# Row sums on one core: contiguous 8 MB loads, and early sums stored in 64-byte runs behind the last loads

## Chip, cores, metric

One core of one Trainium2 chip; the other cores are idle. The metric is the device time of one execution in microseconds (us).

## The reference

```python
batch, seq, dim = 32, 512, 1024
x = np.random.randn(batch, seq, dim).astype(np.float32)     # 67.1 MB
return np.sum(x, axis=-1)                                   # 16,384 sums, 64 KB
```

## The kernel before

Partition p takes 112 successive rows in a first block, then 16 in a last one, always 16 rows (64 KB a partition, 8 MB in all) a load. So in the first seven groups the reads of two neighbouring partitions lie 448 KB apart (below: the pitch); in the last group they lie 64 KB apart, and that group is contiguous.

```python
BLOCKS = (112, 16)
G = 16
...
xpool = ctx.enter_context(tc.tile_pool(name="x", bufs=3))
...
for b, n in enumerate(BLOCKS):
    # x_b: x_flat[r0 : r0 + P*n] as "(p c) d -> p (c d)"; out_b alike
    x_b, out_b, res = block(done * P, n)
    ...
        parts = (0, 1, m) if done + c == 0 else (0, m)       # group 1: one row first, then 15
        for i, k in zip(parts, parts[1:]):
            nc.sync.dma_start(out=xt[:, i * D : k * D], in_=x_b[:, (c + i) * D : (c + k) * D])
        ...                                                  # sums: VectorE; 7 of group 7's rows ScalarE
    if not final:
        for i, k in ((0, 104), (104, P)):                    # 448-byte runs, ScalarE's queue
            nc.scalar.dma_start(out=out_b[i:k], in_=res[i:k])
...
# last group: loads of 9, 4, 2 rows, then 544 and 480 columns of the last row (SyncE's queue)
# sums on both engines, then
nc.sync.dma_start(out=out_b, in_=res)                        # 64-byte runs
```

The first two loads are moved ahead of the start barrier.

Of the kernel before, what the change touches and what calls it, by code (L numbers as in the profile page):

```python
# [1 line left out]

# [4 lines left out]

F32 = mybir.dt.float32
ADD = mybir.AluOpType.add
COPY = mybir.ActivationFunctionType.Copy  # L10
X = mybir.AxisListType.X

BLOCKS = (112, 16)
G = 16
ACT_ROWS = 7
CUT = 544
EARLY = 2


@with_exitstack  # L20
def row_sums(
    ctx: ExitStack,
    tc: tile.TileContext,
    x: bass.AP,
    out: bass.AP,
):
    nc = tc.nc
    P = nc.NUM_PARTITIONS

    x_flat = x.flatten_outer_dims()  # L30
    R, D = x_flat.shape
    C = R // P
    assert R % P == 0 and sum(BLOCKS) == C
    out_flat = out.rearrange("a (b c) -> (a b c)", c=1)

    xpool = ctx.enter_context(tc.tile_pool(name="x", bufs=3))
    rpool = ctx.enter_context(tc.tile_pool(name="res", bufs=1))
    part = rpool.tile([P, 1], F32, name="part")
    seen = rpool.tile([P, 1], F32, name="seen")
    pairs = [rpool.tile([P, D // 2], F32, name=f"pairs{i}") for i in range(3)]  # L40

    def rows_dve(xt, res, j, n, c):
        nc.vector.tensor_reduce(  # L43
            out=res[:, c : c + n],
            in_=xt[:, j * D : (j + n) * D].rearrange("p (j d) -> p j d", d=D),
            axis=X,
            op=ADD,
        )

    def sum_act(v, acc):  # L50
        nc.scalar.activation(out=v, in_=v, func=COPY, accum_out=acc)  # L51

    def rows_act(xt, res, j, n, c):
        for i in range(n):
            sum_act(xt[:, (j + i) * D : (j + i + 1) * D], res[:, c + i : c + i + 1])

    def pairs_dve(xt, a, b, first, acc, pairs):
        h = (a + b) // 2
        nc.vector.tensor_tensor_reduce(  # L59
            out=pairs[:, 0 : h - a], in0=xt[:, a:h], in1=xt[:, h:b], scale=1.0, scalar=first,  # L60
            op0=ADD, op1=ADD, accum_out=acc,
        )

    def block(r0, n):
        x_b = x_flat[r0 : r0 + P * n].rearrange("(p c) d -> p (c d)", p=P)
        out_b = out_flat[r0 : r0 + P * n].rearrange("(p c) -> p c", p=P)
        return x_b, out_b, rpool.tile([P, n], F32, name=f"res{r0}")

    full = C - G
    done = 0  # L70
    for b, n in enumerate(BLOCKS):
        x_b, out_b, res = block(done * P, n)
        final = b == len(BLOCKS) - 1
        whole = n - G if final else n
        c = 0
        while c < whole:
            m = min(G, whole - c)
            xt = xpool.tile([P, G * D], F32, tag="xt", name="xt")
            parts = (0, 1, m) if done + c == 0 else (0, m)
            for i, k in zip(parts, parts[1:]):  # L80
                nc.sync.dma_start(
                    out=xt[:, i * D : k * D], in_=x_b[:, (c + i) * D : (c + k) * D]
                )
            a = ACT_ROWS if done + c + m == full else 0
            rows_dve(xt, res, 0, m - a, c)
            rows_act(xt, res, m - a, a, c + m - a)
            c += m
        if not final:

            for i, k in ((0, 104), (104, P)):  # L90
                nc.scalar.dma_start(out=out_b[i:k], in_=res[i:k])
        done += n

    xt = xpool.tile([P, G * D], F32, tag="xt", name="xt")
    cuts = [0, 9, 13, 15]
    for i, k in zip(cuts, cuts[1:]):
        nc.sync.dma_start(out=xt[:, i * D : k * D], in_=x_b[:, (c + i) * D : (c + k) * D])  # L97
    last = 15 * D
    for i, k in ((0, CUT), (CUT, D)):
        nc.sync.dma_start(  # L100
            out=xt[:, last + i : last + k],
            in_=x_b[:, c * D + last + i : c * D + last + k],
        )

    for i, k in zip(cuts[:2], cuts[1:3]):
        h = (k - i) // 2
        rows_dve(xt, res, i, h, c + i)
        rows_act(xt, res, i + h, k - i - h, c + i + h)
    pairs_dve(xt, 13 * D, 14 * D, 0.0, res[:, c + 13 : c + 14], pairs[2])
    rows_act(xt, res, 14, 1, c + 14)  # L110
    pairs_dve(xt, last, last + CUT, 0.0, part, pairs[0])


    nc.vector.tensor_copy(out=seen, in_=part)  # L114
    pairs_dve(xt, last + CUT, last + D, part, res[:, c + 15 : c + 16], pairs[1])
    nc.sync.dma_start(out=out_b, in_=res)


def kernel(tc: tile.TileContext, x: bass.AP, out: bass.AP):
    row_sums(tc, x, out)  # L120
    tc.close()
    tc.compile()  # L122



    sp = mybir.EngineType.SP
    fn = tc.nc.m.functions[0]
    entry, body = None, None
    for blk in fn.blocks:
        ops = [i for i in blk.instructions if i.engine == sp]  # L130
        if entry is None:
            entry = blk
        elif any(i.opcode == "DMACopy" for i in ops):
            body = blk
            break
    code = list(body.instructions)
    loads = [i for i in code if i.engine == sp][:EARLY]
    for load in loads:
        assert load.opcode == "DMACopy" and not load.sync_info.on_wait
        code.remove(load)  # L140
    body.instructions = code
    code = list(entry.instructions)
    at = next(k for k, i in enumerate(code) if i.engine == sp and i.opcode == "Drain")
    code[at:at] = loads
    entry.instructions = code

# [1 line left out]
_INS = ['x']  # L148
_OUTS = [((32, 512), 'float32')]


# [23 lines left out]
```

## Time and profile before

| | before |
|---|---|
| median of six runs | 162.13 us (162.03 to 162.42) |
| span in the profile | 160.6 us |
| DMA engines on loads | 97.2% of the span |
| VectorE busy | 76% |
| from one group's landing to the next | 19.37 us, 433 GB/s |
| group one landed | 21.98 us |

What bounds the kernel, with the lines of the page, is in the prediction. The trace also records each DMA packet (its queue, start, duration and bytes, but not which of the 16 engines ran it) and each of the 16 completions of a load. "Landed" below is the last of a load's completions, in us from the span's start.

### The profile page before, as it was taken

How to read it: one execution, taken by the hardware profiler on the slowest of the kernel's cores; microseconds unless marked ns; L12 is line 12 of the kernel's file. 1: busy time of each engine (PE TensorE's matmuls, PEld its weight loads, DVE VectorE, ACT ScalarE, POOL GpSimd, SP SyncE). 2: the span in 40 equal slices, each digit the busy share in tenths (PEclk: the TensorE clock that was granted, in tenths of full speed). 3: DMA queues.
4: the chain of work that ended last, by engine and by line, in shares of the span. 5: the costliest groups of instructions: out<-in, count | busy, mean ns of one | idle time of the engine just before them, and what ended most of it. 6: DMA issues, size and time to landing. Idle time of an engine off the chain costs nothing.

```text
span 160.6 us, 120 instructions
## 1 busy us (share of the span) xinstructions
DVE 121.4 (76%) x16; ACT 17.2 (11%) x31; POOL 0.2 (0%) x4
## 2 busy tenths in 40 slices
DVE  0000059997799958999499994999949999598884
ACT  0000000000000000000000000000000000596892
POOL 0000000000000000000000000000000000000000
DMA  9997996996996996996996979979969969998991
GB/s 375 490 398 337 490 522 294 490 522 261 522 506 278 522 506 278 522 506 278 522 506 278 522 326 457 522 310 473 522 294 490 522 261 522 432 432 369 410 402 62
DMA packets 2169, 67.18 MB, mean 418 GB/s; under 512 B 505, under 2 KB 633, under 8 KB 889
## 3 DMA queue, kind: packets, MB, share of 16 engines
q1 hardware_dynamic: 2016, 67.12, 97.2%
q10 hardware_dynamic: 153, 0.06, 0.1%
HBM read 67.11 MB, written 0.07 MB: 418 GB/s over the span
## 4 chain that ended last, share of the span: by engine, by line
DMA 75%; DVE 22%; SPq 0%; issue 0%; DVEq 0%
DMA xt<-in_x_dram 75%; DVE res L43 21%; DVE pairs L59 1%; SPq L97 0%; DVE seen L114 0%; DVE part L59 0%; DVEq L122 0%; DVE res L59 0%
## 5 line engine op out<-in xcount | busy, mean ns | idle before, releaser
L43 DVE TENSOR_REDUCE res<-xt 128x16 f32<-128x16384 f32 (+3 forms) x9 | 119.8, 13309 | 36.6 <-DMA xt<-in_x_dram 36.6
L51 ACT ACT_TABLE_LOAD x1 | 1.3, 1283 | 138.3 <-DMA xt<-in_x_dram 138.3
L51 ACT ACTIVATE xt<-xt 128x1024 f32<-128x1024 f32 x15 | 15.6, 1042 | 2.2 <-DMA xt<-in_x_dram 2.2
L51 ACT ACTIVATION_READ_ACCUMULATOR xt<-xt 128x1 f32 x15 | 2.8, 186 | 0.0
L59 DVE CUSTOM_DVE_ANT_0 pairs<-xt 128x512 f32<-128x512 f32 (+1 forms) x2 | 1.1, 566 | 0.3 <-DMA xt<-in_x_dram 0.3
L59 DVE CUSTOM_DVE_ANT_0 pairs<-xt,part 128x240 f32<-128x240 f32 x1 | 0.5, 467 | 0.0
L114 DVE COPY seen<-part 128x1 f32<-128x1 f32 x1 | 0.2, 153 | 0.0
L59 DVE DVE_READ_ACCUMULATOR2_ANT res<- 128x1 f32 x2 | 0.2, 81 | 0.0
L159 POOL MEMSET const-bfloat16-1.0<- 128x1 bf16 x1 | 0.1, 101 | 0.0
L159 POOL MEMSET const-uint8-127<- 128x1 uint8 x1 | 0.1, 101 | 0.0
L159 POOL MEMSET const-float32-0.0<- 128x1 f32 x1 | 0.1, 98 | 0.2 <-issue 0.2
L159 POOL MEMSET const-float32-1.0<- 128x1 f32 x1 | 0.1, 98 | 0.0
L59 DVE DVE_READ_ACCUMULATOR2_ANT part<- 128x1 f32 x1 | 0.1, 84 | 0.0
## 6 DMA issues: line engine op xcount, KB each, us to landing
xt<-in_x_dram SPq DMA_DIRECT2D x1, 7680.0 KB
xt<-in_x_dram SPq DMA_DIRECT2D x1, 4608.0 KB, 32.4
xt<-in_x_dram SPq DMA_DIRECT2D x1, 2048.0 KB, 36.9
xt<-in_x_dram SPq DMA_DIRECT2D x1, 1024.0 KB, 39.0
xt<-in_x_dram SPq DMA_DIRECT2D x1, 512.0 KB, 3.9
xt<-in_x_dram SPq DMA_DIRECT2D x1, 272.0 KB, 39.1
xt<-in_x_dram SPq DMA_DIRECT2D x1, 240.0 KB, 38.9
xt<-in_x_dram SPq DMA_DIRECT2D x6, 40.9
```

The lines of the kernel that those rows point to most:

```text
L43: nc.vector.tensor_reduce(out=res[:, c : c + n], in_=xt[:, j * D : (j + n) * D].rearrange("p (j d) -> p j d", d=D), axis=X, op=ADD,)
L51: nc.scalar.activation(out=v, in_=v, func=COPY, accum_out=acc)
L59: nc.vector.tensor_tensor_reduce(out=pairs[:, 0 : h - a], in0=xt[:, a:h], in1=xt[:, h:b], scale=1.0, scalar=first, op0=ADD, op1=ADD, accum ...
L114: nc.vector.tensor_copy(out=seen, in_=part)
L159: nc = _bacc.Bacc("TRN2", target_bir_lowering=False, num_devices=1)
```

## The change

Its intent: every load is one unbroken 8 MB of HBM, and the stores leave ScalarE and the middle of the load stream. The price is that group g's 16 sums of a partition are 64 bytes in the output, 8 KB from those of the next group.

```diff
-BLOCKS = (112, 16)
...
+    x_g = x_flat.rearrange("(b p c) d -> b p (c d)", p=P, c=G)
+    out_g = out_flat.rearrange("(b p c) -> p b c", p=P, c=G)
+    res = rpool.tile([P, C], F32, name="res")
...
+        for i, k in ((0, 1), (1, G)) if b == 0 else ((0, G),):
+            nc.sync.dma_start(out=xt[:, i * D : k * D], in_=x_g[b, :, i * D : k * D])
...
-            for i, k in ((0, 104), (104, P)):
-                nc.scalar.dma_start(out=out_b[i:k], in_=res[i:k])
...  (after the last group's loads)
+    for i, k in ((0, 4), (4, B - 1)):
+        nc.sync.dma_start(out=out_g[:, i:k], in_=res_g[:, i:k])
...
-    nc.sync.dma_start(out=out_b, in_=res)
+    nc.sync.dma_start(out=out_g[:, B - 1], in_=res[:, c:C])
```

More of the change, by code (lines that the diff above doesn't have):

```diff
@@ L32, in row_sums @@
     C = R // P
-    assert R % P == 0 and sum(BLOCKS) == C
+    assert R % P == 0 and C % G == 0
     out_flat = out.rearrange("a (b c) -> (a b c)", c=1)
@@ L62, in pairs_dve @@
         )
-    def block(r0, n):
-        x_b = x_flat[r0 : r0 + P * n].rearrange("(p c) d -> p (c d)", p=P)
-        out_b = out_flat[r0 : r0 + P * n].rearrange("(p c) -> p c", p=P)
-        return x_b, out_b, rpool.tile([P, n], F32, name=f"res{r0}")
-    full = C - G
-    done = 0
-    for b, n in enumerate(BLOCKS):
-        x_b, out_b, res = block(done * P, n)
-        final = b == len(BLOCKS) - 1
-        whole = n - G if final else n
-        c = 0
-        while c < whole:
-            m = min(G, whole - c)
-            xt = xpool.tile([P, G * D], F32, tag="xt", name="xt")
-            parts = (0, 1, m) if done + c == 0 else (0, m)
-            for i, k in zip(parts, parts[1:]):
-                nc.sync.dma_start(
-                    out=xt[:, i * D : k * D], in_=x_b[:, (c + i) * D : (c + k) * D]
-                )
-            a = ACT_ROWS if done + c + m == full else 0
-            rows_dve(xt, res, 0, m - a, c)
-            rows_act(xt, res, m - a, a, c + m - a)
-            c += m
-        if not final:
-            for i, k in ((0, 104), (104, P)):
-                nc.scalar.dma_start(out=out_b[i:k], in_=res[i:k])
-        done += n
+    x_g = x_flat.rearrange("(b p c) d -> b p (c d)", p=P, c=G)
+    out_g = out_flat.rearrange("(b p c) -> p b c", p=P, c=G)
+    B = C // G
+    res = rpool.tile([P, C], F32, name="res")
+    for b in range(B - 1):
+        xt = xpool.tile([P, G * D], F32, tag="xt", name="xt")
+        for i, k in ((0, 1), (1, G)) if b == 0 else ((0, G),):
+            nc.sync.dma_start(out=xt[:, i * D : k * D], in_=x_g[b, :, i * D : k * D])
+        a = ACT_ROWS if b == B - 2 else 0
+        rows_dve(xt, res, 0, G - a, b * G)
+        rows_act(xt, res, G - a, a, (b + 1) * G - a)
+    c = (B - 1) * G
+    x_b = x_g[B - 1]
     xt = xpool.tile([P, G * D], F32, tag="xt", name="xt")
@@ L96, in row_sums @@
     for i, k in zip(cuts, cuts[1:]):
-        nc.sync.dma_start(out=xt[:, i * D : k * D], in_=x_b[:, (c + i) * D : (c + k) * D])
+        nc.sync.dma_start(out=xt[:, i * D : k * D], in_=x_b[:, i * D : k * D])
     last = 15 * D
@@ L101, in row_sums @@
             out=xt[:, last + i : last + k],
-            in_=x_b[:, c * D + last + i : c * D + last + k],
+            in_=x_b[:, last + i : last + k],
         )
+    res_g = res.rearrange("p (b c) -> p b c", c=G)
+    for i, k in ((0, 4), (4, B - 1)):
+        nc.sync.dma_start(out=out_g[:, i:k], in_=res_g[:, i:k])
     for i, k in zip(cuts[:2], cuts[1:3]):
```

## The prediction

> **What bounds the kernel now.** I read the views in this order: the busy time by engine, the 40 slices, the stretches between two loads, the chain of waits and the timeline of the end, then the trace's record of each DMA packet.
>
> The page first. The columns of the last line are the rates of the 40 slices.
>
> ```profile
> DVE 121.4 (76%) x16; ACT 17.2 (11%) x31; POOL 0.2 (0%) x4
> ...
> DMA  9997996996996996996996979979969969998991
> GB/s 375 490 398 337 490 522 294 490 522 261 522 506 278 522 506 278 522 506 278 522 506 278 522 326 457 522 310 473 522 294 490 522 261 522 432 432 369 410 402 62
> ...
> q1 hardware_dynamic: 2016, 67.12, 97.2%
> q10 hardware_dynamic: 153, 0.06, 0.1%
> ```
>
> VectorE is busy for 76% and the 16 DMA engines for 97% of the span, nearly all of it on the loads (q1). The digits 6 and 7 and rates that swing between 261 and 522 look like gaps, but are an effect of the slices: a packet holds up to 64 KB, and its bytes are counted in the slice where it is recorded. Stretches from one load's landing to the next (bounds taken from the starts of VectorE's big sums) show it. Columns: stretch and length, busy time of the three engines, clock, DMA share, GB/s.
>
> ```profile
> 41.35:60.72 19.37, 17.22 (x2) 0.00 (x0) 0.00 (x0) 1.00 1.00 433
> 60.72:80.09 19.37, 17.22 (x1) 0.00 (x0) 0.00 (x0) 1.00 1.00 433
> ...
> 138.27:157.80 19.53, 17.60 (x8) 17.19 (x31) 0.00 (x0) 1.00 0.95 402
> ```
>
> A group of 16 rows a partition lands every 19.37 us, with the DMA engines busy all the time. VectorE needs 17.22 us for it and waits 2.15 us each time. The last stretch (402 GB/s) is not slower: 8.39 MB in 19.53 us are 430 GB/s; its first packets were recorded in the stretch ahead. The packets confirm this: a 65,536-byte packet takes 2.418 us (median of 768), and each engine carries eight a group, 8 x 2.418 = 19.34 us, so there is no gap between packets.
>
> The end of the chain of waits (start, length, what):
>
> ```profile
> 117.65 38.95 DMA xt<-in_x_dram
> 156.60 0.02 issue
> 156.62 0.69 DVE pairs L59
> 157.32 0.01 DVE res L59
> 157.32 0.36 DVE pairs L59
> 157.68 0.02 DVE part L59
> 157.70 0.02 issue
> 157.73 0.15 DVE seen L114
> 157.88 0.41 DVE pairs L59
> 158.29 0.01 DVEq L122
> ```
>
> And in the timeline of the end, the last store:
>
> ```profile
> 158.36 0.35 SPq L116 DMA_DIRECT2D out_dram<-res  x1
> ```
>
> The last load lands by the packet records at 157.81, VectorE sums its 240 pairs and the store of the last group's sums goes out at 158.36. Its first packet starts at 159.21, its last completion is recorded at 159.79, and the span ends at 160.6. So the time is: about 1.0 us to the first packet, some 157 us of loads at the engines' full rate, and a tail of 2.8 us. Only something that changes the packets' rate, the slowest engine's work, or this tail can change the end.
>
> **What the Trainium skill says.** All four places are on "DMA: Bandwidth & Descriptors".
> - "Where 436 GB/s comes from" (in "Bandwidth") gives 435.2 GB/s as the ceiling of 16 ports. The trace agrees: 433 GB/s in an undisturbed stretch. A better order of reads in HBM has half a per cent to win at most.
> - "Latency and other measured facts" lists that a pitch from partition to partition of 512 KiB and more, at powers of two, slows copies, and advises padding or tiles laid out contiguously. The first seven loads now have a pitch of 448 KB and get 64 KB. 64 KB is a power of two but below the listed sizes. The trace already has it: the last group of the kernel before is a contiguous 8 MB with 64 KB pitch. Its packets of 36,864 bytes took 1.364 us, 27.0 bytes a ns, against 27.1 for the 65,536-byte ones at 448 KB pitch. That small gap is a fixed cost of about 9 ns a packet, which the two sizes give together.
> - "Specifications" says that transfers under 512 B make the DMA engine read, modify and write. The last store has 64-byte runs already. Its 128 packets are recorded with 8 to 11 ns each, and successive ones on one engine start about 7 ns apart. So no such cost shows there, though that is only 8 packets an engine.
> - "Queues, rings and completion order" says that one engine consumes descriptors in ring order, and that the completion write lands only after every earlier write of that engine. So a slow early store can hold up a later one's completion. Nothing in this trace tests that.
>
> **The change, part by part.**
>
> 1. Loads of the first seven groups: same count, bytes and packets (64 KB a partition), other addresses. By the last group's evidence 0 us; I allow 0.2 us either way, mainly for the first 4 KB packets, which take up to 0.94 us while the transfers start.
>
> 2. The two stores from ScalarE's queue go. They were 128 packets of 448 bytes at 25 ns in the last group. Their 25 completion packets show that they ran on 13 and 12 engines, up to 10 packets an engine. From the landing of the group before to that of the last, the engine that lands first took 19.72 us, the one that lands last 19.55 us. So these stores delayed the engines that were ahead by about 0.17 us and apparently left the slowest alone. The 0.19 us by which the slowest exceeds 19.36 is the cutting of the last load in five: the packet times sum to 2.451 us instead of 2.418 us, eight times, so 0.26 us, about right. Removing the stores wins 0 to 0.05 us. The 0.98 us that ScalarE's queue spent issuing them lay in a wait for data (ACT idles 2.19 us until 149.20).
>
> 3. The new stores: 4 x 128 and 3 x 128 runs of 64 bytes, 896 packets on 16 engines, 56 an engine and two completions. Building the changed kernel shows their place: both on SyncE's queue after the last load, ahead of the last store. The first needs no fresh wait (the load ahead has already waited for its sums). The second waits for group seven's sums on both engines, about 147 us as now. Both are thus issued some 10 us before the loads end, and lie behind them in the same rings. They start on an engine when its last load packet ends, 157.39 on the slowest. At 7 to 14 ns (recorded spacing, and double it) 58 packets take 0.4 to 0.8 us, until 157.8 to 158.2. The last store cannot start before 159.21, because its sums aren't there. The hole between the loads and the last store is 159.21 - 157.39 = 1.82 us, and the new stores fit in it up to 1.82 / 58 = 31 ns a packet. So 0 us on the path; I allow 0.1 us for issue.
>
> 4. VectorE and ScalarE do the same instructions with the same shapes. Writing into one tile of sums brings no new wait: in the built kernel, the sums of the last group wait only for their loads, as before.
>
> Sum: 0 (loads) - 0.02 (old stores) + 0.05 (new stores) = +0.03 us. Predicted 162.1 us.
>
> **The rivals.**
>
> - Short writes to HBM are slow when there are many. Eight packets an engine may be absorbed by a buffer and 56 not. For it: only the last store shows such packets, and the skill warns of them. Against: 7 ns apart, and completion 0.37 us after the last packet. At 60 ns a packet the stores end at 157.39 + 58 x 0.06 = 160.9, the last store comes 1.7 us later, and the time is 163.8. To be slower by 2% (165.3 us), 3.2 us more are needed, so (1.82 + 3.2) / 58 = 87 ns a packet, eight to twelve times the recorded spacing.
> - The queue fills: the long row of descriptors behind the loads stops SyncE's issue, and the last store goes out late. Against: the loads drain from 149 on, and the last store is issued only at 158.36. If it had to wait for room it would cost some tenths, 162.5.
> - The 64 KB pitch makes the engines collide in HBM when seven groups run so. Against: the last group. Were 1% lost, it would be seven times 0.19, +1.4 us: 163.5.
> - Contiguous reads gain. The floor is 433 to 435 GB/s, 0.5% of 155 us, so -0.7 us at the very best: 161.4. The unbroken rows of packets speak against it.
>
> **Range and chances.** The runs of before lie within 0.11 us. Below, only the start and a hair of rate can win: 161.6. Above, the first three rivals in mild form add up to 0.9 us: 163.0. Faster by over 2% (under 158.9) is beyond the ceiling of the transfers: 0.01. Slower by over 2% needs the first rival in strong form, or two per cent of load rate: 0.04. The rest, 0.95, is within 2%.
>
> **What would show it right or wrong.** Right: stretches of 19.37 us at 433 GB/s; the old stores' queue gone and q1 with 896 64-byte packets and 32 completions more; these packets between about 157 and 158.3; the last store's instruction near 158.4 with 1.4 us to landing. Wrong: longer stretches or longer 65,536-byte packets (step 1, the pitch); small packets beyond 159.2 or the last store with more than 1.4 us to landing (step 3, short writes); SyncE's last issue well after VectorE's last sum (the queue); sums of the last group waiting for a store (step 4).

## More of the kernel before

All runs quoted here are at full clock. The experiments, e1 to e12, ran on four different chips, so each ratio compares only runs of the same rounds on one chip; the kernel before had medians of 162.04 to 162.23 us there.

## The result, and the profile after

| | before | after |
|---|---|---|
| median of six runs | 162.13 us | 162.77 us (162.55 to 163.01) |
| span in the profile | 160.6 us | 161.2 us |
| group one landed | 21.98 us | 22.41 us |
| last load landed | 157.80 us | 158.43 us |

The ratio is 1.0037 (95% interval 1.0024 to 1.0051): within 2%, but a real loss of 0.6 us. Ratios are the mean time of one kernel's fast runs over that of the other's of the same rounds, so not quite the ratio of the medians quoted. The profiled run of the changed kernel was its slowest of six (163.01); that of the kernel before, at 162.37 us, was also above its median.

From the page of the changed kernel, its slices and queues; q10, the queue of ScalarE's stores, is gone, and q1 has 928 packets more (896 of 64 bytes and 32 completions):

```profile
DMA  9979997997997997997998998998998999998992
...
q1 hardware_dynamic: 2944, 67.18, 97.5%
```

The stretches from one landing to the next, as read in the kernel before:

```profile
41.78:61.14 19.36, 17.22 (x2) 0.00 (x0) 0.00 (x0) 1.00 1.00 433
61.14:80.54 19.40, 17.22 (x1) 0.00 (x0) 0.00 (x0) 1.00 1.01 432
80.54:100.02 19.48, 17.22 (x2) 0.00 (x0) 0.00 (x0) 1.00 1.00 431
...
138.76:158.43 19.67, 17.74 (x8) 17.16 (x31) 0.00 (x0) 1.00 0.96 399
```

The middle is as it was, to a few hundredths (the longest stretch, 19.48 us, was 19.46 us before). The first sum of VectorE shows where the time went. Timeline (start, length, engine, operation, idle before), first of the kernel before:

```profile
22.08 17.22 DVE L43 TENSOR_REDUCE res<-xt 128x16 f32<-128x16384 f32 x1 [22.08 <-DMA xt<-in_x_dram]
```

and of the changed kernel:

```profile
22.51 17.22 DVE L42 TENSOR_REDUCE res<-xt 128x16 f32<-128x16384 f32 x1 [22.51 <-DMA xt<-in_x_dram]
...
119.55 29.42 SPq L93 DMA_DIRECT2D out_dram<-res  x2
...
158.45 0.47 DVE L58 CUSTOM_DVE_ANT_0 pairs<-xt,part 128x240 f32<-128x240 f32 x1
158.85 0.08 DVE L58 DVE_READ_ACCUMULATOR2_ANT res<- 128x1 f32 x1
159.00 0.34 SPq L106 DMA_DIRECT2D out_dram<-res  x1
```

0.43 of the 0.6 us are already there when group one has landed, long before any store. The end, from the last load's landing to the end of the span, is 2.8 us in both. The two new stores are issued far ahead (the line that begins at 119.55; it covers the wait of the second for group seven's sums). Their 896 packets run from 157.16 to 158.27, before the last store needs the engines.

To see what happens in group one I use an "excess": for all packets of one size, the time beyond the median of that size, summed and divided by 16, so the time that a mean DMA engine loses. For group one's first transfer (4 KB packets) and second one (61,440 bytes) it was 468 and 10 ns in the kernel before, 760 and 144 ns in the changed one. The later groups' 65,536-byte packets show no increase (407 and 384 ns in sum over six groups).

The first theory, S+E: the 64 KB pitch makes the start slower (0.41 us), and the 64-byte packets delay the completion of the last load (0.13 us: from the end of the last 1,920-byte packet to the landing it was 0.42 us before and 0.56 after). The main rival T: the stores carry the loss and the start is chance.

### The profile page after: what moved, and what is told of

Its sections match the earlier page's. It is cut to its first block, busy times and chain, and to the rows that moved or that the text cites. A ratio compares the mean times of both kernels' runs of the same rounds, so it can differ in the third digit from the quotient of the medians.

```text
span 161.2 us, 121 instructions
## 1 busy us (share of the span) xinstructions
DVE 121.5 (75%) x16; ACT 17.2 (11%) x31; POOL 0.2 (0%) x4
## 4 chain that ended last, share of the span: by engine, by line
DMA 75%; DVE 22%; SPq 1%; issue 0%; DVEq 0%
DMA xt<-in_x_dram 75%; DVE res L42 21%; SPq L81 1%; DVE pairs L58 0%; SPq L84 0%; DVEq L112 0%
```

## The experiments

In the experiments that read or write wrong places, instructions, bytes and packets are the changed kernel's or the one's before, apart from the stores in e3 and e4. In the rounds of e1 to e4, one of the eleven runs of the kernel before took 163.31 us (the others 161.93 to 162.29). It widens these four intervals and lowers their ratios by 0.0007, and it shows that the kernel before, too, can lose a microsecond in a single execution.

**The first transfer alone, both ways.** The changed kernel with its first transfer at 448 KB pitch (e1):

```diff
+    x_old = x_flat[0 : P * 112].rearrange("(p c) d -> p (c d)", p=P)
...
-            nc.sync.dma_start(..., in_=x_g[b, :, i * D : k * D])
+            src = x_old if (b, i) == (0, 0) else x_g[b]
+            nc.sync.dma_start(..., in_=src[:, i * D : k * D])
```

> The changed kernel, but its very first transfer (one row a partition, 4 KB packets) reads at the old pitch of 448 KB; wrong on purpose in the first sum of each run of group one. Theory S (the start: 4 KB packets at 64 KB pitch come in slower, 0.41 us of the 0.6): group one lands near 22.0 us as in the kernel before (22.4 in the changed one), 4 KB packets take about 28 us in sum instead of 32.5, time 162.35, ratio 1.0015. Rival T (all of it is the tail, the start was chance): start varies without order, time stays at 162.7 (1.0037). Rival P (the second transfer's 64 KB pitch makes the start slow): landing stays at 22.4, time 162.7.

Measured: 162.45 us, ratio 1.0022 (0.9997 to 1.0047). Group one landed at 21.90, 4 KB excess 338 ns, but the second transfer's excess was 328 ns. The point estimate is some 40% below the changed kernel's, but the interval holds the whole loss and none of it.

The kernel before with the first transfer at 64 KB pitch (e2):

```diff
+    x_new = x_flat[0 : P * G].rearrange("(p c) d -> p (c d)", p=P)
...
+                src = x_new if (done + c, i) == (0, 0) else x_b
```

> The kernel before, but its very first transfer reads at 64 KB pitch (wrong in one sum of each first run). Theory S: group one lands 0.3 to 0.4 us later, near 22.4, and the time is 162.5 (1.0025). Rivals T and P: 22.0 and 162.13 (1.000).

Measured: 162.31 us against 162.09 us, ratio 1.0011 (0.9986 to 1.0036), landing 21.78. The point estimate is under a third of the loss, but the interval reaches from none of it to nearly all, so this run alone does not settle what the first transfer costs.

**The stores alone, both ways.** The changed kernel without them (e3):

```diff
-    for i, k in ((0, 4), (4, B - 1)):
-        nc.sync.dma_start(out=out_g[:, i:k], in_=res_g[:, i:k])
```

> The changed kernel without the two stores of 64-byte runs; 7 of 8 groups stay unwritten, wrong on purpose. Theory S+E (0.41 us at the start, 0.13 us because the completions of the last load come later when 64-byte packets stand behind them): from the last 1,920-byte packet's end to the last load's last completion 0.43 us as in the kernel before (0.56 in the changed one), time 162.6 (1.0030). Rival T (stores carry most of the loss): time 162.2 (1.0005). Rival C (the tail's 0.13 us has nothing to do with the stores): 0.56 us stays, time 162.75.

Measured: 162.70 us, ratio 1.0039 (1.0012 to 1.0066); taking the stores out wins nothing that shows. Group one landed at 22.22 (excess 462 and 422 ns). The last load's completion came 0.40 us after its last packet.

The loads of before with the stores of the change (e4):

```diff
-            for i, k in ((0, 104), (104, P)):
-                nc.scalar.dma_start(out=out_b[i:k], in_=res[i:k])
...  (after the last group's loads)
+    for i, k in ((0, 4), (4, 7)):
+        nc.sync.dma_start(out=out_g[:, i:k], in_=res_g[:, i:k])
```

> The loads of the kernel before, with the two stores of 64-byte runs behind the last loads on SyncE's queue (the sums land at wrong rows, on purpose). Theory S+E: group one lands at 22.0, completion of the last load 0.5 to 0.56 us after its last packet, time 162.25 (1.0008). Rival T: 162.7 (1.0035).

Measured: 162.10 us against 162.09 us, ratio 0.9996 (0.9972 to 1.0020). The stores cost nothing that shows, at most 0.2% (0.3 us) by the interval; they cannot carry the whole loss, and rival T has fallen. Theory E has nearly fallen too. In the eight profiles with these stores (the changed kernel, e1, e4, e5, e6, e7, e9, e10) the completion took 0.42 to 0.60 us after the last packet, in four without (before, e2, e3, e8) 0.40 to 0.42. So a delay of 0 to 0.2 us seems to be there, but the time of e4 does not show it.

So the loads' addresses are the cause, and theory G took the place of S+E: group one in both its transfers.

**Group one whole.** The changed kernel, group one at 448 KB pitch (e5):

```diff
+            src = x_old if b == 0 else x_g[b]
```

> The changed kernel, but both transfers of group one read at the old pitch of 448 KB (wrong sums in group one on purpose). Theory G (the whole loss arises while group one is loaded, in both its transfers, from the 64 KB pitch): group one lands at 21.6 to 22.0, few slow 61,440-byte packets (excess under 60 ns an engine, against 144 to 422 with the 64 KB pitch), time equal to the kernel before, 162.1 (ratio 0.999 to 1.001). Rival R (the other six groups' 64 KB pitch costs too): 162.3 or more.

Measured: 162.62 us, ratio 1.0019 (1.0007 to 1.0031). Group one was healed in the profile (21.82, excess of the second transfer 2 ns), but the five times fell in two heaps, 162.26 and 162.28 against 162.62, 162.68 and 162.78. By the point estimate only half the loss is gone (the intervals overlap), so rival R seems to hold in part.

The kernel before, group one at 64 KB pitch (e8):

```diff
+                src = x_new if done + c == 0 else x_b
```

> The kernel before, with both transfers of group one at 64 KB pitch (wrong sums on purpose). Theory G: the whole loss appears, group one lands at 22.2 to 22.4, time 162.7 (1.0037). Rival R (the groups after it are needed too): at most 162.4.

Measured: 162.71 us against 162.19 us, ratio 1.0032 (1.0020 to 1.0044); landing 22.24, excess 742 and 194 ns. Nearly the whole loss, from group one alone, with everything else as before. Its first sum in the timeline:

```profile
22.34 17.22 DVE L43 TENSOR_REDUCE res<-xt 128x16 f32<-128x16384 f32 x1 [22.34 <-DMA xt<-in_x_dram]
```

The changed kernel, only the second transfer at 448 KB pitch (e6):

```diff
+            src = x_old if (b, i) == (0, 1) else x_g[b]
```

> The changed kernel, with only the second transfer of group one (60 KB packets) at 448 KB pitch. Theory G, the second transfer carrying about half: 162.35 (1.0015), excess of the 61,440-byte packets under 60 ns an engine. Rival F (only the first transfer's pitch counts, the second suffers from the order in which the first leaves the engines): excess stays at 150 to 400 and time at 162.7.

Measured: 162.55 us, ratio 1.0021 (1.0009 to 1.0033); excess 605 and 3 ns. The slow packets of the second transfer do go with its own pitch; rival F has fallen. The landing, 22.32, was late all the same. In e2 all of group one has the same addresses as here, and it landed at 21.78. The first sums of e2 and of e6:

```profile
21.88 17.22 DVE L43 TENSOR_REDUCE res<-xt 128x16 f32<-128x16384 f32 x1 [21.88 <-DMA xt<-in_x_dram]
```

```profile
22.41 17.22 DVE L42 TENSOR_REDUCE res<-xt 128x16 f32<-128x16384 f32 x1 [22.41 <-DMA xt<-in_x_dram]
```

So at the same addresses two single landings can lie 0.54 us apart, as much as the whole effect looked for. One profile of the start therefore proves little; the times of e8 and the many profiles taken together (below) carry the reading.

**Is it the power of two?** Group one at 68 KB (e7):

```diff
+    x_old = x_flat[0 : P * 17].rearrange("(p c) d -> p (c d)", p=P)
...
+            src = x_old if b == 0 else x_g[b]
```

> The changed kernel, with both transfers of group one at a pitch of 68 KB (64 KB plus one row; wrong sums on purpose). Theory A (the engines, in step at the start, meet in HBM because 64 KB is a power of two): the slow packets go, as at 448 KB, time 162.1 (1.000). Rival N (what hurts is that the partitions lie close together in HBM, whatever the pitch): excess 150 to 400 ns an engine stays, time 162.6 to 162.8 (1.0035).

Measured: 162.83 us, ratio 1.0037 (1.0024 to 1.0050). The profiled run was its fastest (162.28): landing 21.91, excess 546 and 22 ns, as at 448 KB. The profile speaks for theory A, the median against it. The groups after the first still read at 64 KB pitch here, so the slow runs may have lost their time later, as e10 below did; none of them was profiled. Not settled.

**What happens in the slow runs of e5.** The same kernel, twice more, for another profile (e9, e10):

> The same kernel as e5_group1_448, for another profile: its five times fell in two heaps (162.26 and 162.28; 162.62 to 162.78), and only a run of the lower heap was profiled. Theory L (with group one at 448 KB, the loss can come later, when group two first reads at 64 KB pitch while the engines are still in step): in a run of the upper heap group one lands at 21.6 to 22.0 and the 65,536-byte packets of group two or three show an excess of 150 to 400 ns an engine. Rival S (the start itself varies): group one lands at 22.2 or later, no excess afterwards. A run near 162.3 tells nothing of this.

> As e9_again_group1_448, once more, to raise the chance of a profile of the upper heap: theory L an excess of 150 to 400 ns an engine in group two or three, rival S a late landing of group one (22.2 or later).

Measured: 162.30 and 162.67 us, and 162.56 twice (ratios 1.0027 and 1.0032; the kernel before had 162.04 us on this chip). With e5's these are nine times with a mean of 162.52 us. The profile of e9 was of the lower heap; that of e10 (162.56 us) was of the upper. Its stretches:

```profile
99.04:118.41 19.37, 17.22 (x1) 0.00 (x0) 0.00 (x0) 1.00 1.01 433
118.41:138.05 19.64, 17.22 (x1) 0.00 (x0) 0.00 (x0) 1.00 0.93 404
138.05:149.31 11.26, 9.76 (x1) 8.66 (x15) 0.00 (x0) 1.00 0.97 406
```

Its timeline shows VectorE's sums (and the waits in brackets) at the same place:

```profile
21.72 17.22 DVE L42 TENSOR_REDUCE res<-xt 128x16 f32<-128x16384 f32 x1 [21.72 <-DMA xt<-in_x_dram]
...
118.43 17.22 DVE L42 TENSOR_REDUCE res<-xt 128x16 f32<-128x16384 f32 x1 [2.15 <-DMA xt<-in_x_dram]
138.06 9.76 DVE L42 TENSOR_REDUCE res<-xt 128x9 f32<-128x9216 f32 x1 [2.42 <-DMA xt<-in_x_dram]
149.32 4.42 DVE L42 TENSOR_REDUCE res<-xt 128x4 f32<-128x4096 f32 x1 [1.50 <-DMA xt<-in_x_dram]
```

Group one came early (21.62), but group seven took 19.64 us and the 9-row load of the last group 11.26, where the kernel before has 19.35 and 10.91: 0.6 us lost late. In the packets it is a spell in which all 16 engines slow together: excess 224 ns in group seven and 357 ns in the 36,864-byte packets, none of which was slow in the kernel before. So theory L is right that the loss can come later, but wrong on where (group two or three); rival S fell with this run. The other profiles of changed kernels whose first transfer was put at 448 KB show it too: in group seven and the 9-row load together the excess is 365 ns in e1, 324 in e5 and 275 in e9 (runs of the lower heap), 581 in e10, and at most 184 in the ten others. So what the start no longer loses seems to be lost in part later, while the groups read at 64 KB pitch; four profiles suggest that, and no run tests it. Spells are not of the 64 KB pitch alone: the profiled run of the kernel before has one of 195 ns in group five, though a loose one (14 slow packets strewn over 84 to 92 us) that put off the landing by only 0.1 us.

**A version to beat both, and short writes put to the test.** A correct kernel whose first transfer is the first 128 rows (pitch 4 KB, contiguous), the rest of the first block at 444 KB pitch (e11):

```diff
-BLOCKS = (112, 16)
+FIRST = 1
+BLOCKS = (111, 16)
...
+            if head:
+                nc.sync.dma_start(out=xt[:, 0 : head * D], in_=x_1)
...
+            if head:                     # after group 1's sums
+                for i, k in ((0, 104), (104, P)):
+                    nc.scalar.dma_start(out=out_1[i:k], in_=res_1[i:k])   # 4-byte runs
```

> A correct version of the kernel before whose first transfer is a contiguous 512 KB (the first 128 rows, one a partition, pitch 4 KB) and whose other rows up to the last group have a pitch of 444 KB, no multiple of 64 KB; the first rows' sums are stored in 4-byte runs early on ScalarE's queue. Theory A (the start suffers from pitches that are multiples of 64 KB, 448 KB included): excess of the 4 KB packets falls from 340 to 580 to under 300 ns an engine, time 161.9 (0.9987). Rival N (reads that lie close together are slow at the start): excess as at 64 KB pitch, 460 to 760, time 162.3 (1.001).

Measured: 163.37 us, ratio 1.0095 (1.0066 to 1.0123), correct. The start was better, as theory A wants (4 KB excess 238 ns, landing 21.61), though the second transfer's excess was 192 ns, which a pitch of 444 KB should not have by theory A. Rival N has fallen for the first transfer: no reads lie closer together than these, yet group one came as early as in the best of the other profiles (21.60; in e12 below, with the same loads, 299 ns and 21.65). But group two lost a microsecond:

```profile
21.63 16.15 DVE L44 TENSOR_REDUCE res<-xt 128x15 f32<-128x15360 f32 x1 [17.16 <-DMA xt<-in_x_dram]
42.04 17.22 DVE L44 TENSOR_REDUCE res<-xt 128x16 f32<-128x16384 f32 x1 [4.26 <-DMA xt<-in_x_dram]
61.40 17.22 DVE L44 TENSOR_REDUCE res<-xt 128x16 f32<-128x16384 f32 x1 [2.14 <-DMA xt<-in_x_dram]
```

VectorE waits 4.26 us instead of 2.1. In the packets 16 overlapping 65,536-byte packets, so one on every engine, begun at 30.55 to 30.96 us, took 3.1 to 3.9 us instead of 2.42, while the last 12 of the 128 sums are written as 4-byte packets (30.54 to 30.89). The 116 before them, from 9.40 us on, passed without such a stall; why only the last met one is open.

The same with the 4-byte store behind the last loads (e12):

```diff
-                for i, k in ((0, 104), (104, P)):
-                    nc.scalar.dma_start(out=out_1[i:k], in_=res_1[i:k])
...  (after the last group's loads)
+    nc.sync.dma_start(out=out_1, in_=res_1)
```

> e11_first_rows_contiguous with its store of 4-byte runs moved behind the last loads on SyncE's queue (a correct version, candidate). In e11 all 16 engines lost 0.92 us in one packet each near 30.6 us, in group two, while the 4-byte packets ran. Theory W (4-byte writes among the loads caused it): group two shows an excess under 60 ns an engine, group seven lands at 137.7 to 138.0, time 161.9 to 162.2 (0.999 to 1.001). Rival Q (the 444 KB pitch causes it): excess near 1000 ns an engine stays in group two, time 163.2 (1.007 or more).

Measured: 165.56 us, ratio 1.0205 (1.0191 to 1.0219), correct. The first half of theory W holds: group two's excess is 39 ns, group seven lands at 137.75, and the last load at 157.38. With the 4-byte writes moved, the stall is gone from group two, at the same pitch (one profile of each). Its time is 3.4 us above the range that theory W gave, though, for the writes hit the tail. Timeline, the last store's issue and landing, and SyncE's wait in this kernel:

```profile
158.02 0.34 SPq L120 DMA_DIRECT2D out_dram<-res  x1
```

```profile
out_dram<-res SPq DMA_DIRECT2D x1, 8.0 KB, 5.6
```

```profile
SPq L126 <- DMA out_dram<-res: 5.0, 1, 5.0
```

and the same landing and wait in the changed kernel:

```profile
out_dram<-res SPq DMA_DIRECT2D x1, 8.0 KB, 1.4
```

```profile
SPq L112 <- DMA out_dram<-res: 0.8, 1, 0.8
```

The 4-byte packets left the engines by 157.07 like any others, but the last of the store's completions came at 162.88. The last store of 64-byte runs, whose packets were out at 159.07, had its last completion only at 163.58: 5.6 us after issue instead of 1.4. So here packet times did not show what the short writes cost; their completions did.

No version beat the kernel before.

## Why the prediction was right, and where its sum was off

The time (162.77 us in 161.6 to 163.0) and the class were right. The sum of +0.03 us was not: +0.6 us. That the range held is partly luck: its upper end summed mild forms of three rivals, of which the short writes and the full queue did not come, while the start, where the loss came, had been allowed 0.2 us. Nor did any of its signs of being wrong look at the landing of group one.

- *What bounds the kernel.* Right. The middle stretches stayed at 19.35 to 19.48 us (19.35 to 19.46 before), and VectorE waited for the loads throughout, so nothing hid a late load. The spread of 0.11 us that the range starts from is that of three runs; six runs of the kernel before spread over 0.39 us.
- *Step 1, the loads: "By the last group's evidence 0 us; I allow 0.2 us either way, mainly for the first 4 KB packets".* This is the term that was mis-sized. It named half of the right place, and 0.2 should have been 0.43 in the pair of profiles and 0.55 in the mean of all. Over all profiles group one landed at 21.98, 21.60, 21.82, 21.70 and 21.62 with both transfers at 448 KB pitch (mean 21.74), and at 22.41, 22.22 and 22.24 with both at 64 KB (mean 22.29). The excess of its two transfers summed to 423 to 582 ns against 884 to 936 ns, 0.44 us more in the mean, of which 0.21 us lie in the second transfer, which the prediction did not name. The evidence from the last group was taken 138 us into an unbroken stream, and from one profile. It held for the middle of the stream, but said nothing of the start; and e10 shows that the same last group can lose 0.35 us in another run.
- *Step 2, the old stores.* "0 to 0.05 us" is not contradicted: e4 takes them out and puts the new ones in at no difference (0.9996), but its interval of 0.4 us either way cannot show so little. That the old stores delayed the engines that are ahead fits e3, which has neither kind: there the first engine took 19.57 us from landing to landing, against 19.72 before, and the last one 19.54 against 19.55. The cutting of the last load, 0.26 us for a measured 0.19, is only roughly right.
- *Step 3, the new stores.* Right. On the slowest engine they ran from the end of its last load packet, 157.87, to 158.27, 7 ns a packet, before the last store's first at 159.84. e3 and e4 agree that they cost nothing that the times show. The rival of slow short writes does not hold for these 64-byte runs. e12 shows that it exists for 4-byte runs, and its completions (162.88 for the early store, 163.58 for the last) fit the way the prediction named: an early store's outstanding writes hold up the completion of a later one. No run isolates that.
- *Step 4, no new waits.* Right; VectorE's waits before its sums of the last group are 1.15, 0.47 and 0.22 us, all for loads, with 1.16, 0.47 and 0.26 before.
- *The pitch rival* was closest, but not as put there (1% of every group). The loss comes mostly in group one, or, where that was healed, in a spell later.

Shown: the loads' addresses carry the loss, and the stores do not (e3, e4); group one at 64 KB pitch suffices for nearly all of it (e8). Not shown: why. The parts do not add up (e8 +0.5 us; group one healed in e5, e9, e10 still +0.4 us; together +0.6), so healing group one is not enough. That would fit engines that meet in HBM while they run in step, and lose the step by it, but no run measures that, and e7 leaves open whether the power of two matters. Why the spells come in some executions and not in others is open as well.

## What to carry to other kernels

In this kernel the DMA engines had no gap (433 GB/s in an undisturbed stretch), so "more contiguous" had next to nothing to win. In such a case look for what the new addresses do to the start of the stream and to single slow spells, and don't take the late part of a stream as evidence for its beginning. Here stores of 64-byte runs behind the last loads were free: their packets fitted into the hole that the last sums leave, and their completions were quick. Judge short writes by their completion, and look at more than one profile when times fall in two heaps or an effect is no larger than the spread of single runs.

## What the Trainium skill lacked or had wrong

- "DMA: Bandwidth & Descriptors", "Latency and other measured facts": the entry on power-of-two pitches begins at 512 KiB and speaks of a lasting rate. Here 64 KB against 448 KB left the rate in the middle alone (431 to 434 GB/s) and delayed the landing of the first 8 MB by 0.55 us (22.29 against 21.74, means of three and five profiles). Its advice to lay tiles out contiguously is given for those pitches; followed at 448 KB, it made this kernel 0.4% slower.
- The same page, "Specifications": one threshold of 512 B for read-modify-write. 64-byte runs went at 7 ns a packet, and the store of the last sums landed 1.4 us after issue. 128 runs of 4 bytes held completions until 162.88, almost 6 us after their packets, and the next store with them (5.6 us). In the midst of the loads they went with a stall of 0.92 us on all 16 engines at once. That page does not tell the two sizes apart, and none has the time to completion of runs as short as either.
- The same page, "Where 436 GB/s comes from", says in one sentence that for transfers between HBM and SBUF the HBM side of about 358 GB/s binds. A core that streams alone ran at 433 GB/s here; "HBM Reference", "Specifications (TRN2)", has the right picture for this case.
- No page speaks of spells in which all engines slow together for a few packets. One cost 0.6 us in e10 (excess of 224 ns in group seven and 357 ns in the 9-row load); four profiles here have 275 to 581 ns in these two loads.
